# Scans that take the carry over 257 columns, gated outputs loaded during their projection, other waits in the background jobs, and first operands prepared one at a time

## The chip, the cores and the metric

The kernel runs on one core of one Trainium2 chip. A core has five engines with instruction queues of their own: TensorE for matrix products (PE in the profile, its weight loads PEld), VectorE (DVE), ScalarE (ACT), GpSimd (POOL) and SyncE (SP), which here issues nearly all DMA transfers. An engine works through its own queue in order and waits at an instruction until the data and buffers it needs are free. The metric is the time of the program on the device in microseconds (us), the median of several runs; lower is better.

## The reference

One decoder layer on a sequence of 1024 positions and 2048 channels, all in float32. It normalizes `x`, projects it with `w_in` to 6656 columns, and runs two groups of 16 heads of width 64: stick-breaking attention (`sb`) and sliding-window attention with four key/value heads, a position bias and a sink (`sw`). Each group's output is normalized over its 1024 columns, multiplied by a gain and by `silu(z)` of its own gate projection, and both together go through `w_out`, a norm and the residual.

```python
# stick breaking, for s < t:
A[t, s] = sigmoid(z_ts) * prod_{s < j < t} (1 - sigmoid(z_tj))
# the layer
u = rmsnorm(h, norm_pre)
q_sb, k_sb, v_sb, z_sb, q_sw, k_sw, v_sw, z_sw = split(u @ w_in)
o_sb = rmsnorm(stick_breaking(q_sb, k_sb, v_sb), gn_sb) * silu(z_sb)
o_sw = rmsnorm(sliding_window(q_sw, k_sw, v_sw, sinks, rel_bias), gn_sw) * silu(z_sw)
y = concatenate([o_sb, o_sw]) @ w_out
h = h + rmsnorm(y, norm_post)
```

The sequence is stored back to front, so the product over later keys in the reference becomes a running product from left to right: a scan.

## The kernel before

**Precision.** A float32 product is made from three faster ones: each operand is split into a high part (a cast on ScalarE, L133, L545, L747, L774) and the rest (a subtraction on VectorE, L135, L546, L748, L775), and TensorE adds high by high, high by low and low by high (L122, L872).

**Phase 1: projections.** `w_in` is cut into 52 blocks of 128 columns. `proj` (L435) makes one: four groups `kg` of four 128-row tiles, for both halves `h` of the 1024 positions, 96 matmuls of 512 columns. The list `work` (L700) fixes their order: window heads first, then queries, keys and values of the eight stick-breaking pairs with the gate projections `z_sw` and `z_sb` between them, and at the end six `z_sb` alone. After each block its `done` function empties the accumulators.

**Attention in between.** After every few matmuls `proj` calls `step` (L252), which starts at most one piece of attention (`advance`, L152) and then lets the background jobs go on. A unit of stick-breaking attention (`unit_sb`, L495) covers 256 queries, as two blocks of 128, by 256 keys: its first part computes logits, the two sigmoids into `m` and `beta` (L515, L517), and two scans over 256 columns (L526), one per block of queries. The tile `m` has 257 columns; column 0 is the running product so far. In the first unit of a row of units GpSimd sets it to 1 (L520); in every later one GpSimd copies it from column 256 of the unit before (L524). Then `beta` is multiplied by `m` shifted by one column (L530). The second part transposes on TensorE (L537, L126) and splits; the third multiplies by the values, and the output goes to the tensors `od` in device memory.

**The gate.** `evac_z` (L404) ends a z projection. For each half it loads the attention output from `od` (two parts, L408, one buffer with the tag `or`), adds the parts on GpSimd (L410), computes `silu(z)` times the gain (L366, L413, L414), multiplies by the output (L415), squares the output on GpSimd and adds that to the group's sum (L419, L421, L422), and stores the product to `ogd` (L423). `group_rms` (L425) turns the sum into one over the root mean square, in rows of 512 positions (L430, L431); for the window heads that happens 12 planner-microseconds after the last `z_sw`, for the others during the first product of phase 2.

**Background jobs.** 80 `sum_job`s add or subtract blocks of `w_out` (two loads, one operation on GpSimd, one store); eight `scale_job`s then multiply the gated window outputs by their norm row, store that to `ogs`, subtract the halves and store that to `w21`. Two chains run them, one in a tile `bg`, one in `row_sw` until that tile is needed for the norm. The number after each `yield` is the least time until the job's next step.

**What sets the order.** The program counts `pe_time`, the time TensorE should have needed for the matmuls written so far; `defer`, the lags of the units and the waits of the jobs are all in these planner-microseconds. Matmuls of phase 1 and the steps of background jobs keep their written order; other instructions are ordered on their engines by a scheduler that simulates them when the program is built, with earlier-written ones preferred.

**Phase 2.** The output projection is done as seven products of quarter matrices (the idea of Strassen and Winograd), each over `e = 0..7` and two column halves `dc`. Its first operands are the scaled window outputs: `open_ph2` (L781), called before the last two projections, finishes what is deferred and all background jobs, frees the tiles of phase 1, and prepares all eight operands: `x_source` (L753) loads one from `ogs`, with two buffers, and `x_split` (L771) splits it. The weights are loaded by `load_wo` (L720) and split by `split_wo` (L731), the first eight with two buffers for the parts.

## Time and profile before

| | |
|---|---|
| median of 3 runs | 1875.68 us (1872.5 to 1877.07) |
| the profiled execution | 1870.6 us, span of its instructions 1868.9 us |
| mean granted TensorE clock | 0.987 |
| TensorE busy | 1794.2 us, 96% of the span |
| VectorE, ScalarE, GpSimd busy | 1263.6, 772.7 and 586.6 us |
| HBM traffic | 219.42 MB read, 91.23 MB written |

In a row of the profile, L526 is line 526 of the kernel; `m_sb<-m_sb,zero` names what is written and what is read; x192 counts instructions. In a timeline the first two numbers are the start and the duration in us, and the bracket at the end tells how long the engine had been idle and whose work ended that. SPq stands for SP's queue issuing a transfer. PEclk is the clock that TensorE was granted, as a share of full speed. A busy TensorE can still be slow, when the clock is low.

### The profile page before, as it was taken

The numbers are of one execution on the slowest core, as the hardware profiler recorded it, in microseconds if no ns is written. First come the engines' busy times: TensorE is split into PE (matmuls) and PEld (weight loads), VectorE is DVE, ScalarE is ACT, GpSimd is POOL, SyncE is SP. The second block draws the span as 40 slices with busy tenths as digits, with TensorE's granted clock in tenths as the row PEclk, the third lists the DMA queues.
The fourth block names the chain that finished last, engine by engine and source line by source line (L and its number), as shares of the span: only waits on it lengthen the run. The fifth ranks groups of instructions, "written<-read, shape, count | busy, mean of one in ns | idle before, by whom it ended". The sixth has DMA issues, their size and how long they took to land. (4 is left out here: it accounts for less than half of the span.)

```text
span 1868.9 us, 27447 instructions
## 1 busy us (share of the span) xinstructions
PE 1794.2 (96%) x9046; PEld 1498.4 (80%) x9046; DVE 1263.6 (68%) x1976; ACT 772.7 (41%) x1664; POOL 586.6 (31%) x680
## 2 busy tenths in 40 slices
PE   8999999999999999999999989999999958999997
PEld 7788888878888878887888868888878846888886
DVE  7568842888387686785776767767688536655776
ACT  7345521445244343442433425434344214434432
POOL 0111121112234253253342332223444553403623
PEclk9999999999999999999999999999999979999999
DMA  7546775566646465555555553544534477534475
GB/s 228 195 141 189 200 211 149 159 191 201 201 142 177 139 186 169 167 156 157 161 168 164 155 161 106 151 120 144 157 110 141 134 243 240 163 108 136 135 246 188
DMA packets 205421, 312.50 MB, mean 167 GB/s; under 512 B 26176, under 2 KB 85728, under 8 KB 205152
## 3 DMA queue, kind: packets, MB, share of 16 engines
q1 hardware_dynamic: 203216, 307.61, 54.9%
q10 hardware_dynamic: 2064, 3.15, 0.5%
q8 instruction: 72, 1.18, 0.3%
q14 instruction: 69, 0.57, 0.1%
HBM read 219.42 MB, written 91.23 MB: 166 GB/s over the span
## 5 line engine op out<-in xcount | busy, mean ns | idle before, releaser
L526 DVE TENSOR_TENSOR_SCAN m_sb<-m_sb,zero 128x256 f32<-128x256 f32 x192 | 165.0, 900 | 47.3 <-ACT m_sb L515 45.5
L872 PE MATMUL y<-wohi,x 128*128 128x512 f32 x448 | 144.3, 399 | 15.1 <-ACT x L774 13.5
L515 ACT ACTIVATE m_sb<-z_sb 128x512 f32<-128x512 f32 x160 | 96.2, 601 | 147.4 <-PE z_sb L122 136.0
L521 POOL TENSOR_SCALAR_AFFINE_SELECT b_sb<-b_sb 128x512 f32<-128x512 f32 x64 | 48.9, 764 | 328.0 <-ACT b_sb L517 325.9
L530 DVE TENSOR_TENSOR b_sb<-b_sb,m_sb 128x512 f32<-128x512 f32 x160 | 137.3, 858 | 19.2 <-POOL b_sb L521 7.1
L545 ACT CAST wh_sb<-wt_sb 128x512 fp32r<-128x512 f32 (+1 forms) x160 | 87.1, 544 | 130.4 <-PE wt_sb L126 130.0
L526 DVE TENSOR_TENSOR_SCAN m_sb<-m_sb,mask 128x256 f32<-128x256 f32 x128 | 114.3, 929 | 38.8 <-ACT m_sb L515 38.1
L872 PE MATMUL y<-wohl,x 128*128 128x512 f32 x576 | 132.8, 389 | 1.5 <-DVE wohl L748 1.5
L546 DVE TENSOR_TENSOR wl_sb<-wt_sb,wh_sb 128x512 fp32r<-128x512 f32 (+1 forms) x160 | 100.5, 630 | 47.8 <-ACT wh_sb L545 47.4
L872 PEld LDWEIGHTS y<-wohl,x 128*128 128x128 f32 x576 | 108.0, 188 | 24.3 <-DVE wohl L748 1.9
L872 PEld LDWEIGHTS y<-wohi,x 128*128 128x128 f32 x448 | 86.2, 193 | 34.8 <-ACT x L774 13.9
L122 PE MATMUL p_zsb<-xh,wlo_zsb 128*128 128x512 f32 x256 | 101.7, 397 | 5.4 <-DVE wlo_zsb L135 5.4
L122 PE MATMUL p_vsb<-xh,wlo_vsb 128*128 128x512 f32 x256 | 101.5, 397 | 5.0 <-DVE wlo_vsb L135 5.0
L122 PE MATMUL p_ksb<-xh,whi_ksb 128*128 128x512 f32 x256 | 104.4, 408 | 0.4 <-ACT whi_ksb L133 0.4
L122 PE MATMUL p_zsw<-xh,whi_zsw 128*128 128x512 f32 x256 | 104.7, 409 | 0.0
L122 PE MATMUL p_qsb<-xh,whi_qsb 128*128 128x512 f32 x256 | 104.6, 409 | 0.0
L122 PE MATMUL p_zsb<-xh,whi_zsb 128*128 128x512 f32 x256 | 103.9, 406 | 0.0
L122 PE MATMUL p_vsb<-xh,whi_vsb 128*128 128x512 f32 x256 | 103.9, 406 | 0.0
L126 PE MATMUL wt_sb<-ident,b_sb 128*128 128x128 f32 x576 | 89.5, 273 | 14.0 <-DVE b_sb L530 14.0
L126 PEld LDWEIGHTS wt_sb<-ident,b_sb 128*128 128x128 f32 x576 | 72.4, 141 | 37.9 <-issue 17.6
L122 PE MATMUL p_zsw<-xh,wlo_zsw 128*128 128x512 f32 x256 | 101.4, 396 | 0.0
L122 PE MATMUL p_vsb<-xl,whi_vsb 128*128 128x512 f32 x256 | 101.3, 396 | 0.0
(243 smaller groups left out, 5125.8 us busy)
## 6 DMA issues: line engine op xcount, KB each, us to landing
bg<-in_w_out SPq DMA_DIRECT2D x86, 256.0 KB, 4.2
woraw<-wsum SPq DMA_DIRECT2D x80, 256.0 KB, 3.2
row_sw<-in_w_out SPq DMA_DIRECT2D x74, 256.0 KB, 4.5
wsum<-bg SPq DMA_DIRECT2D x43, 256.0 KB, 2.6
kh<-kd SPq DMA_DIRECT2D x160, 64.0 KB, 2.8
kl<-kd SPq DMA_DIRECT2D x160, 64.0 KB, 2.7
wsum<-row_sw SPq DMA_DIRECT2D x37, 256.0 KB, 2.6
q_sw<-qd SPq DMA_DIRECT2D x64, 128.0 KB, 3.3
```

Source lines behind the costliest of these rows:

```text
L122: tc.keep_in_program_order(nc.tensor.matmul(ps, a, b, start=start, stop=stop))
L126: tc.keep_in_program_order(nc.tensor.transpose(ps, a, ident))
L515: nc.scalar.activation(m[:, :, 1:257], z, AF.Sigmoid, scale=-SCALE)
L521: nc.gpsimd.affine_select(out=beta, in_=beta, compare_op=ALU.is_gt, fill=0.0, base=0, pattern=[[-P, 2], [1, 256]], channel_multiplier=-1)
L526: nc.vector.tensor_tensor_scan(m[:, tb, 1:257], m[:, tb, 1:257], mask[:, P - P * tb:P - P * tb + 256] if prev is None else zero.to_broadca ...
L530: nc.vector.tensor_mul(beta, beta, m[:, :, 0:256])
L545: nc.scalar.copy(wh[:, :k], pt[:, :k])
L546: nc.vector.tensor_sub(wl[:, :k], pt[:, :k], wh[:, :k].bitcast(F32))
L872: nc.tensor.matmul(ps, xt[:, a, tcols], w[b][:, cols], start=first and n == 0, stop=last and n == 2)
```

## The change

- `unit_sb`: column 0 of `m` is set to 1 in every unit. Where there is a unit before, the scan runs over all 257 columns and starts from that unit's last column, so GpSimd copies nothing.
- `evac_z`: the load and the addition of the first half move into the projection, ahead of its third group of weights (`mid`, `early`). The second half is loaded once the first has been used, and its multiplication, squares and store are deferred by 6 planner-microseconds, except in the last projection. The squares move from GpSimd to ScalarE.
- `group_rms` makes both products first and hands back the reciprocals as pieces: eight of 128 columns for the window heads, deferred one by one; four of 256 for the others, second half first, one for each `e` from 3 to 6. Its call in phase 2 moves from `e == 3` to `e == 2`.
- Background jobs: waits of 8, 6 and 6 in place of 9, 6 and 7 in a `sum_job`; 7, 4, 4, 4, 4 in place of 9, 6, 7, 6, 7 in a `scale_job`; the chains begin at 112 and 122 in place of 130 and 140. The scale jobs are queued 14.5 planner-microseconds after the window heads' norm.
- Phase 2: the eight first operands become a background job (`prepare_x0`) with a wait of 5 between loads, finished after the last projection.

```diff
@@ -223,31 +223,31 @@
         def run(t):
             BG(nc.sync.dma_start(t[:, 0, :], w_view(a, e, cols)))
             BG(nc.sync.dma_start(t[:, 1, :], w_view(b, e, cols)))
-            yield 9.0
+            yield 8.0
             BG((nc.gpsimd.tensor_add if sign > 0 else nc.gpsimd.tensor_sub)(t[:, 0, :], t[:, 0, :], t[:, 1, :]))
             yield 6.0
             BG(nc.sync.dma_start(wsum[i][e][:, cols], t[:, 0, :]))
-            yield 7.0
+            yield 6.0
...
     def scale_job(e):
         def run(t):
             f = t.rearrange("p a n -> p (a n)")
             BG(nc.sync.dma_start(f, ogd[8 + e]))
-            yield 9.0
+            yield 7.0
             BG(nc.gpsimd.tensor_mul(f, f, row_sw))
-            yield 6.0
+            yield 4.0
             BG(nc.sync.dma_start(ogs[e], f))
-            yield 7.0
+            yield 4.0
             BG(nc.gpsimd.tensor_sub(t[:, 0, :], t[:, 1, :], t[:, 0, :]))
-            yield 6.0
+            yield 4.0
             BG(nc.sync.dma_start(w21[e], t[:, 0, :]))
-            yield 7.0
+            yield 4.0
         return run
 
     jobs.extend(sum_job(i, e, dc) for i in W_SUMS for dc in range(2) for e in range(8))
-    open_chain(row_sw, 130.0)
-    open_chain(at.tile([P, 2 * HALF], F32, tag="bg", name="bg", bufs=1), 140.0)
+    open_chain(row_sw, 112.0)
+    open_chain(at.tile([P, 2 * HALF], F32, tag="bg", name="bg", bufs=1), 122.0)
 
...
@@ -401,38 +401,53 @@
 
     accs = {}
 
-    def evac_z(ps, name, tile_i, gain, grp):
+    early_o = {}
+
+    def load_o(name, tile_i, h):
+        o2 = stg.tile([P, 2, HALF], F32, tag="or", name=f"or_{name}_{h}", bufs=1)
+        nc.sync.dma_start(o2, od[tile_i][:, :, h * HALF:(h + 1) * HALF].rearrange("r p t -> p r t"))
+        nc.gpsimd.tensor_add(o2[:, 0, :], o2[:, 0, :], o2[:, 1, :])
+        return o2[:, 0, :]
+
+    def evac_z(ps, name, tile_i, gain, grp, last=False):
+        zf, sg = [], []
         for h in range(2):
+            zf.append(scaled(ps[h], name, h))
+            sg.append(stg.tile([P, HALF], F32, tag="sg", name=f"sg_{name}_{h}"))
+            nc.scalar.activation(sg[h], zf[h], AF.Sigmoid)
+            nc.vector.scalar_tensor_tensor(zf[h], zf[h], gain, sg[h], op0=ALU.mult, op1=ALU.mult)
+        if tile_i % 8 == 0:
+            accs[grp] = stg.tile([P, S], F32, tag="acc", name=f"acc_{grp}", bufs=1)
+
+        def gate(h, o):
             cols = slice(h * HALF, (h + 1) * HALF)
-            o2 = stg.tile([P, 2, HALF], F32, tag="or", name=f"or_{name}_{h}", bufs=1)
-            nc.sync.dma_start(o2, od[tile_i][:, :, cols].rearrange("r p t -> p r t"))
-            o = o2[:, 0, :]
-            nc.gpsimd.tensor_add(o, o, o2[:, 1, :])
-            zf = scaled(ps[h], name, h)
-            sg = stg.tile([P, HALF], F32, tag="sg", name=f"sg_{name}_{h}")
-            nc.scalar.activation(sg, zf, AF.Sigmoid)
-            nc.vector.scalar_tensor_tensor(zf, zf, gain, sg, op0=ALU.mult, op1=ALU.mult)
-            nc.vector.tensor_mul(zf, zf, o)
+            nc.vector.tensor_mul(zf[h], zf[h], o)
+            nc.sync.dma_start(ogd[tile_i][:, cols], zf[h])
             if tile_i % 8 == 0:
-                if h == 0:
-                    accs[grp] = stg.tile([P, S], F32, tag="acc", name=f"acc_{grp}", bufs=1)
-                nc.gpsimd.tensor_mul(accs[grp][:, cols], o, o)
+                nc.scalar.square(accs[grp][:, cols], o)
             else:
-                nc.gpsimd.tensor_mul(sg, o, o)
-                nc.gpsimd.tensor_add(accs[grp][:, cols], accs[grp][:, cols], sg)
-            nc.sync.dma_start(ogd[tile_i][:, cols], zf)
-
-    def group_rms(grp, row):
-        for h in range(2):
+                nc.scalar.square(sg[h], o)
+                nc.gpsimd.tensor_add(accs[grp][:, cols], accs[grp][:, cols], sg[h])
+
+        gate(0, early_o.pop(name))
+        o1 = load_o(name, tile_i, 1)
+        if last:
+            gate(1, o1)
+        else:
+            defer(6.0, lambda: gate(1, o1))
+
+    def group_rms(grp, row, width, order=(0, 1)):
+        ps = {h: pz(f"rms_{grp}_{h}") for h in order}
+        for h in order:
             cols = slice(h * HALF, (h + 1) * HALF)
-            ps = pz(f"rms_{grp}_{h}")
-            mm(ps, ones, accs[grp][:, cols], start=True, stop=True)
-            nc.scalar.activation(row[:, cols], ps, AF.Sqrt, bias=eps, scale=1.0 / 1024)
-            nc.vector.reciprocal(row[:, cols], row[:, cols])
+            mm(ps[h], ones, accs[grp][:, cols], start=True, stop=True)
+            nc.scalar.activation(row[:, cols], ps[h], AF.Sqrt, bias=eps, scale=1.0 / 1024)
+        parts = [row[:, h * HALF + c:h * HALF + c + width] for h in order for c in range(0, HALF, width)]
+        return [lambda r=r: nc.vector.reciprocal(r, r) for r in parts]
 
...
-    def proj(b, name, nxt=None):
+    def proj(b, name, nxt=None, mid=None):
...
@@ -441,6 +456,8 @@
         ps = [pproj(f"p_{name}_{h}") for h in range(2)]
         for kg in range(4):
             wh, wl = splits.pop(0)
+            if kg == 2 and mid is not None:
+                mid()
             if kg < 3:
                 splits.append(get(b, name, kg + 1))
             elif nxt is not None:
@@ -516,16 +533,17 @@
             beta = at.tile([P, 2, 256], F32, tag="beta", name=f"b_{un}", bufs=3)
             nc.scalar.activation(beta, z, AF.Sigmoid, scale=SCALE)
             prev = grp.get("prev")
+            nc.gpsimd.memset(m[:, :, 0:1], 1.0)
             if prev is None:
-                nc.gpsimd.memset(m[:, :, 0:1], 1.0)
                 nc.gpsimd.affine_select(out=beta, in_=beta, compare_op=ALU.is_gt, fill=0.0, base=0,
                                         pattern=[[-P, 2], [1, 256]], channel_multiplier=-1)
-            else:
-                nc.gpsimd.tensor_copy(m[:, :, 0:1], prev[:, :, 256:257])
             for tb in range(2):
-                nc.vector.tensor_tensor_scan(m[:, tb, 1:257], m[:, tb, 1:257],
-                                             mask[:, P - P * tb:P - P * tb + 256] if prev is None else zero.to_broadcast([P, 256]),
-                                             m[:, tb, 0:1], ALU.mult, ALU.max)
+                if prev is None:
+                    nc.vector.tensor_tensor_scan(m[:, tb, 1:257], m[:, tb, 1:257], mask[:, P - P * tb:P - P * tb + 256],
+                                                 m[:, tb, 0:1], ALU.mult, ALU.max)
+                else:
+                    nc.vector.tensor_tensor_scan(m[:, tb, :], m[:, tb, :], zero.to_broadcast([P, 257]),
+                                                 prev[:, tb, 256:257], ALU.mult, ALU.max)
             grp["prev"] = m
             nc.vector.tensor_mul(beta, beta, m[:, :, 0:256])
             me["w"] = beta
@@ -675,16 +693,25 @@
             if p == 7:
                 def rms():
                     close_chain(chains[0])
-                    group_rms("sw", row_sw)
-                    jobs.extend(scale_job(e) for e in range(8))
+                    for n, piece in enumerate(group_rms("sw", row_sw, 128)):
+                        defer(2.0 + 1.5 * n, piece)
+                    defer(14.5, lambda: jobs.extend(scale_job(e) for e in range(8)))
                 defer(12.0, rms)
         return f
 
     def done_z_sb(p):
         def f(ps):
-            drain(f"sb{p}")
-            evac_z(ps, f"zsb{p}", p, gsb[:, p:p + 1], "sb")
+            evac_z(ps, f"zsb{p}", p, gsb[:, p:p + 1], "sb", p == NPAIR - 1)
         return f
+
+    def early(name, tile_i):
+        def f():
+            assert not left.get(f"sb{tile_i}", 0)
+            early_o[name] = load_o(name, tile_i, 0)
+        return f
+
+    mids = {f"zsw{p}": early(f"zsw{p}", 8 + p) for p in range(NPAIR)}
+    mids.update({f"zsb{p}": early(f"zsb{p}", p) for p in range(NPAIR)})
 
...
@@ -785,13 +812,22 @@
         ph2.append(ctx.enter_context(tc.tile_pool(name="at2", bufs=2, reuse_waits="tile")))
         ph2.append(ph2[0].tile([P, D], F32, tag="gp", name="gp", bufs=1))
         nc.sync.dma_start(ph2[1], g_post.partition_broadcast(P))
-        xs.extend(x_split(0, e, x_source(0, e)) for e in range(8))
+        chains.append(dict(buf=None, at=pe_time[0], job=prepare_x0()))
+
+    def prepare_x0():
+        src = []
+        for e in range(8):
+            src.append(x_source(0, e))
+            if e:
+                xs.append(x_split(0, e - 1, src[e - 1]))
+            yield 5.0
+        xs.append(x_split(0, 7, src[7]))
 
     for n, (b, name, done) in enumerate(work):
         nxt = work[n + 1][:2] if n + 1 < len(work) else None
...
-        ps = proj(b, name, nxt)
+        ps = proj(b, name, nxt, mids.get(name))
         if n == len(work) - 3:
             drain(f"sb{NPAIR - 1}")
         if nxt is None:
@@ -800,6 +836,7 @@
         if n == len(work) - 3:
             open_ph2()
 
+    background(True)
     at2, gp = ph2
     row_sb = rstd
 
@@ -896,8 +933,10 @@
                 split_wo(k0 + e + 6)
                 for tb in range(4):
                     mm_out(pss[tb], xs[e], tb, w_ready[k0 + e], whole, e == 0, e == 7)
-                if i == 0 and dc == 0 and e == 3:
-                    group_rms("sb", row_sb)
+                if i == 0 and dc == 0 and e == 2:
+                    pieces_rms = group_rms("sb", row_sb, 256, (1, 0))
+                if i == 0 and dc == 0 and 2 < e < 7:
+                    pieces_rms[e - 3]()
                 if i == 0 and dc == 1:
                     load_b(1, e)
                 if i == 1 and dc == 0:
```

## The prediction

> **What bounds the kernel now.** I read first the page's busy shares, then the list of what TensorE waited for, then stretches of one fortieth of the span.
>
> ```profile
> span 1868.9 us, 27447 instructions
> PE 1794.2 (96%) x9046; PEld 1498.4 (80%) x9046; DVE 1263.6 (68%) x1976; ACT 772.7 (41%) x1664; POOL 586.6 (31%) x680
> ...
> PE wt_sb L126 <- DVE b_sb L530: 14.0, 7, 3.6
> PE y L872 <- ACT x L774: 13.5, 1, 13.5
> ...
> PE p_zsb L122 <- DVE wlo_zsb L135: 5.4, 1, 5.4
> PE o_sb L122 <- DVE wl_sb L546: 5.2, 6, 1.7
> PE y L872 <- DVE wolo L748: 5.0, 2, 4.7
> PE p_vsb L122 <- DVE wlo_vsb L135: 5.0, 1, 5.0
> ```
>
> TensorE runs 96% of the span and the change leaves its matmuls as they are, so only TensorE's idle time, and the slow matmuls after it, can be won. These six rows, all in stages that the change touches, sum to 48.1 us. How much the idle time costs beyond itself is in the granted clock:
>
> ```profile
> 654.10:700.80 46.70, 43.51 (x229) 36.51 (x228) 39.35 (x49) 19.61 (x38) 24.77 (x31) 0.96 0.65 186
> 840.90:887.70 46.80, 43.21 (x215) 36.04 (x214) 27.84 (x38) 13.99 (x28) 15.56 (x22) 0.96 0.52 157
> 1074.60:1121.30 46.70, 40.18 (x191) 32.38 (x190) 29.29 (x31) 13.49 (x24) 16.85 (x21) 0.93 0.54 161
> ...
> 1495.10:1541.80 46.70, 27.10 (x98) 20.95 (x98) 14.32 (x20) 7.99 (x13) 23.55 (x16) 0.75 0.72 244
> 1541.80:1588.60 46.80, 40.88 (x159) 31.43 (x158) 31.93 (x27) 21.81 (x38) 18.66 (x12) 0.92 0.74 239
> 1588.60:1635.30 46.70, 46.70 (x207) 38.66 (x206) 30.14 (x34) 18.96 (x34) 21.91 (x14) 1.00 0.53 163
> ```
>
> The columns are the stretch, its length, then busy time and count of PE, PEld, DVE, ACT, POOL, then the TensorE clock, DMA share and GB/s. A stretch of undisturbed 512-column matmuls holds 207 of them, 46.7 / 207 = 0.226 us each. The two stretches around the change of phase hold 98 and 159: (109 + 48) x 0.226 = **35.4 us** lost there, the slow clock included. In the stick-breaking stage the clock of 0.96, 0.96 and 0.93 costs about 0.04 x 46.7 = 1.9, 1.9 and 0.07 x 46.7 = 3.3 us more than the waits.
>
> **Part 1, the gate of each z projection.** One of the sixteen, in DVE's, POOL's and PE's order of time:
>
> ```profile
> 841.59 0.72 DVE L414 SCALAR_TENSOR_TENSOR u_zsw<-u_zsw,gsw,sg_zsw 128x512 f32<-128x512 f32 x1
> ...
> 848.63 0.69 DVE L415 TENSOR_TENSOR u_zsw<-u_zsw,or_zsw 128x512 f32<-128x512 f32 x1 [5.12 <-POOL or_zsw L410]
> 849.24 3.13 DVE L526 TENSOR_TENSOR_SCAN m_sb<-m_sb,zero 128x256 f32<-128x256 f32 x2
> ...
> 847.31 1.29 POOL L410 TENSOR_TENSOR or_zsw<-or_zsw 128x512 f32<-128x512 f32 x1 [4.67 <-DMA or_zsw<-od]
> 848.68 1.55 POOL L421 TENSOR_TENSOR sg_zsw<-or_zsw 128x512 f32<-128x512 f32 x1
> ...
> 853.32 0.45 PE L126 MATMUL wt_sb<-ident,b_sb 128*128 128x128 f32 x1 [3.59 <-DVE b_sb L530]
> ...
> L526 DVE TENSOR_TENSOR_SCAN m_sb<-m_sb,zero x192: 718/742/1776, 518.0 to 1452.8; 128x256 f32<-128x256 f32 x192
> ...
> or_zsw<-od SPq DMA_DIRECT2D x16, 512.0 KB, 5.4
> ...
> L300 ACT ACTIVATE xsq<-xraw 128x512 f32<-128x512 f32 x30 | 17.8, 623 | 4.0 <-DVE acc_x L301 4.0
> L133 ACT CAST whi_zsb<-wraw_zsb 128x512 fp32r<-128x512 f32 x32 | 19.9, 622 | 41.0 <-PE p_zsb L122 30.0 <-issue 5.1 <-PE p_vsb L122 2.8
> ```
>
> The second half's load cannot start until the first half leaves the one `or` buffer. DVE reaches the second gate, stands 5.12 us, and all behind it is late; then its two scans take 3.13 us in place of 2 x 0.742 while POOL squares beside them; PE stops for 3.59 us. The wait list's 14.0 + 5.2 us are mostly stalls of this shape. With the two clock losses of 1.9 this term holds 19.2 + 3.8 = **23 us**.
>
> The change loads the first half in mid-projection, squares on ACT, and puts the second gate 6 planner-microseconds later. One planner-microsecond is about 1.19 us here (worked out in part 2), so the second gate stands about 7.1 us after the projection. In the rows above it was ready 848.63 - 841.59 = 7.0 us after the second half's silu, which itself comes some 2 us, three operations of about 0.7, behind the projection's end: a gate as late as this, the worst of its kind, still waits about 2 of its 5.1 us; with the load's median of 5.4 us most others are covered. I take a quarter left, **17 us won**; the bounds are 0 (the gate stands before its data as often as today) and 23.
>
> What the edit adds is behind TensorE: 32 squares on ACT, 0.62 us each by the row of x's squares, 20 us on an engine 41% busy, and taken off POOL. The early load of 512 KB goes to SP ahead of a quarter's weight loads; the cast row of the z weights names no wait for their load among its three longest, so it costs nothing while that lead lasts. If each of the 16 made one quarter's weights 2 us late it would be 32 us; I take 0. What is queued behind the new waiting instruction matters more: the second half's square now sits in ACT's order, with the weight casts behind it. Where the load is late, ACT stops as well as DVE.
>
> **Part 2, the pace of the weight sums, and the group norm of the window heads.**
>
> ```profile
> L227 POOL TENSOR_TENSOR bg<-bg x43: 1262/1296/1777, 168.2 to 1273.5; 128x512 f32<-128x512 f32 x43
> L227 POOL TENSOR_TENSOR row_sw<-row_sw x37: 1285/1303/1752, 154.5 to 1094.8; 128x512 f32<-128x512 f32 x37
> L238 POOL TENSOR_TENSOR bg<-bg,row_sw x8: 2346/2400/2772, 1293.6 to 1518.8; 128x1024 f32<-128x1024 f32 x8
> ...
> 1103.95 3.34 DVE L431 RECIPROCAL row_sw<-row_sw 128x512 f32<-128x512 f32 x1
> ...
> 1108.59 0.80 PE L122 MATMUL p_vsb<-xh,wlo_vsb 128*128 128x512 f32 x1 [5.03 <-DVE wlo_vsb L135]
> ```
>
> One chain made 37 sums, 36 steps of 9 + 6 + 7 = 22 planner-microseconds, in 1094.8 - 154.5 = 940.3 us: 26.1 us a step, hence 26.1 / 22 = 1.19. At 20 a step takes 23.7 us; begun 18 x 1.19 = 21 us earlier, both chains fit 2 x (940 + 21) / 23.7 = 81 sums before 1095, where 80 are wanted. So the eight scale jobs no longer queue behind sums until 1273.5: they start near 1115 (the change gives the norm 14.5 planner-microseconds first) and, at 23 planner-microseconds (27 us) each in place of 35, end near 1335 rather than in the last two projections (the last multiply is at 1518.8). By itself this moves nothing on TensorE's path; it is what frees part 3. Denser sums may add or save a microsecond in the window stage: -1 to +3, taken as 0.
>
> The norm's reciprocal is split into eight pieces of 3.34 / 4 = 0.84 us, spread apart. The term is the wait of 5.03 and 3.3 of clock, 8.3 us. ACT's table load and roots stay, and a piece can still push a split: I leave 2.3, about three pieces, **6 won**; bounds 0 and 8.3.
>
> **Part 3, the end of the projections and the first product.**
>
> ```profile
> 1507.83 0.69 DVE L415 TENSOR_TENSOR u_zsb<-u_zsb,or_zsb 128x512 f32<-128x512 f32 x1 [10.79 <-POOL or_zsb L410]
> ...
> 1526.16 0.32 SPq L244 DMA_DIRECT2D w<-bg  x1
> ...
> 1528.61 0.92 SPq L765 DMA_DIRECT2D xs<-ogs  x2
> ...
> 1536.00 1.27 ACT L774 CAST x<-xs 128x512 fp32r<-128x512 f32 x2 [5.62 <-DMA xs<-ogs]
> ...
> 1536.67 0.80 PE L872 MATMUL y<-wohi,x 128*128 128x512 f32 x1 [13.53 <-ACT x L774]
> 1557.55 0.50 PE L872 MATMUL y<-wohi,x 128*128 128x512 f32 x1 [0.88 <-ACT wohi L747]
> ...
> 1534.23 0.69 DVE L415 TENSOR_TENSOR u_zsb<-u_zsb,or_zsb 128x512 f32<-128x512 f32 x1 [4.37 <-POOL or_zsb L410]
> ...
> 1566.45 6.57 DVE L431 RECIPROCAL rstd<-rstd 128x512 f32<-128x512 f32 x2 [3.92 <-ACT rstd L430]
> ```
>
> Today the last scale jobs are forced out at the end, the last store of theirs, at 1526.16, stands ahead in SP's queue, the first x operand is asked for at 1528.61, and TensorE waits 13.53 us and then crawls at a lower clock as x pairs trickle in. The stall of 10.79 us is a gate behind POOL's scale jobs and makes the 5.4 us in the first list. After the change the scale jobs are long done; the eight x operands are asked for one every 5 planner-microseconds, 40 in all, and the two projections that remain are 2 x 96 x 0.226 = 43 us of TensorE's time. So the first product starts as the projections end.
>
> What is late next: the weight splits of the first product have two buffers, so one lasts 12 x 0.226 = 2.7 us. The wait for wohi (0.88) and the wolo that followed it (5.0 - 4.7 = 0.3) stay, 1.2. The last gate is not deferred: today's wait of 4.37 less the 2.7 us in hand is 1.7, and I allow as much again for a lower clock. The 6.57 us of reciprocal become four pieces of 1.64 with splits between them: 1.5. Together about 6 of the 35.4 stay: **29 us won**; bounds 19 (the 1.2, a gate's wait of 4.4 and the reciprocal's of 4.7 as today, each with 3 of clock, are 16 left) and 34.
>
> **Part 4, the scan.**
>
> ```profile
> L524 POOL COPY m_sb<-m_sb 128x2 f32<-128x2 f32 x96 | 50.1, 522 | 117.8 <-DVE m_sb L526 105.7 <-ACT wh_sb L545 8.8 <-ACT b_sb L517 2.6
> ...
> L520 POOL MEMSET m_sb<- x64: 93/98/109, 1.9 to 1453.9; 128x2 f32 x64
> ```
>
> One more column is 742 / 256 = 3 ns on 192 scans, 0.6 us of DVE. POOL loses 50.1 us of copies and gains 96 x 0.098 = 9.4 of memsets. More to the point, POOL no longer stands in its order for the scan before (105.7 us), so its adds for the gates come sooner. None of it is on TensorE's path alone: 0, bounds 0 and +2 of gain, within part 1.
>
> **The sum.** 17 + 6 + 29 = 52 us off the profiled execution's 1870.6 (its span 1868.9 and 1.7 around it): 1818.6. That execution lies 5.1 us under the median of the runs, 1875.68; against the median I expect 1875.7 - 52 = 1823.7, **1824**.
>
> **The rivals.**
>
> *More comes.* Nothing of the stalls stays but the first weights' 1.2: 23 + 8.3 + 34.2 = 65.5, **1810**. For it: every one of the waits has its named cause removed. Against: the order on the engines is replanned, and a plan's loads are faster than the 5.4 us seen here. 15%.
>
> *The wait of the second half stays.* The deferred gates still stand before their data, now ACT with DVE: part 1 gives 4, part 3 its lower bound of 19: 4 + 6 + 19 = 29, **1847**. For it: 4.67 us of POOL's waiting for that load above, and one buffer still. Against: the 7.1 us of delay. 21%.
>
> *The operands are not ready after all.* The sums just miss 1095 (81 places for 80), or the buffers of the second phase come free only with the last units, so x is prepared at the end as today; half of part 3 goes: 17 + 6 + 14.5 = 37.5, **1838**. 9%.
>
> *ACT changes tables for each square* (slower than before). The profile's table loads:
>
> ```profile
> L515 ACT ACT_TABLE_LOAD x2 | 2.6, 1283 | 0.0
> ```
>
> If squares need another table than the sigmoids on both sides of them, each costs ACT two loads, 2 x 1.283 = 2.57 us, in front of the sigmoids and casts that feed PE. 28 of the 32 squares lie ahead of the last two projections, among stick-breaking units; DVE's stall of 5.12 gave PE 3.59, so the 2.57 would give 1.8 and, more often than before, a clock loss; at 2.57 a square, 28 x 2.57 = 72 against the 52 won: **1896**. It decides from 52 / 28 = 1.9 us a square. Against it: L300 squares x at the start, and no load carries that line. 4%. [...]
>
> **How the numbers follow.** The forecast, 1815 to 1833, has 46%; the rivals 15, 21, 9 and 4; another 5% lies around no change (4) or worse (1), by weights late behind the early loads or a worse plan. The range 1808 to 1850 takes in the first three rivals and leaves out the slower cases and some of the tails, under 20%. A measurement of this kernel tells about 0.3%, 5.6 us, from no change. Faster by more 91%, within 4%, slower 5%.
>
> **What would show it.** In the changed profile: the wait of y for ACT's x (13.5) gone and both 46.7 us stretches near 200 matmuls; the last multiply by `row_sw` before 1350; the gate's multiply without a wait on POOL's add over 2 us except at the last projection; table loads still seven; no PE wait of 5 us after the window norm. I am wrong if the first product still waits over 5 us, if PE's waits for b_sb and wl_sb stay above 10, or if ACT waits at the new squares.

## The result, and the profile after

Over four runs each, the changed kernel takes 1820.97 us at the median (1817.14 to 1825.41) and the kernel before 1874.09 (1870.83 to 1877.07): a ratio of **0.9718**, 95% interval 0.9689 to 0.9746, or 53 us less. The forecast was 1824. The profiled execution of the new kernel is the longest of its four, 1825.41 us; so its span, 1823.7 us, lies 45.2 us under the span before, and not 53.

The page of the kernel after, and its list of what TensorE waited for (total, times, longest):

```profile
PE 1786.3 (98%) x9046; PEld 1493.2 (82%) x9046; DVE 1242.3 (68%) x1984; ACT 787.2 (43%) x1696; POOL 496.2 (27%) x648
...
PE wt_sb L126 <- DVE b_sb L548: 3.0, 2, 2.0
...
PE o_sb L122 <- DVE wl_sb L564: 2.4, 2, 1.2
...
PE y L909 <- DVE wolo L775: 1.8, 2, 1.5
PE p_zsb L122 <- ACT whi_zsb L133: 1.4, 1, 1.4
PE p_zsb L122 <- DVE wlo_zsb L135: 1.3, 2, 0.7
```

The six waits on which the forecast was built summed to 48.1 us. The waits for `b_sb` and `wl_sb` are now 5.4 (19.2 before), those of the last projections for their weights 2.7 (5.4), `wolo` 1.8 (5.0). The wait of the first product for `x` (13.5) and that of `p_vsb` (5.0) are not in the list any more. The prediction's stretches but the last, which was undisturbed before too, now of the kernel after:

```profile
654.10:700.80 46.70, 44.73 (x238) 37.86 (x237) 39.24 (x49) 22.43 (x44) 19.14 (x30) 0.96 0.63 177
840.90:887.70 46.80, 46.80 (x244) 39.53 (x243) 29.16 (x42) 16.50 (x33) 12.84 (x23) 1.00 0.60 178
1074.60:1121.30 46.70, 46.70 (x238) 38.70 (x237) 34.62 (x49) 20.27 (x37) 12.44 (x22) 1.00 0.46 142
1495.10:1541.80 46.70, 44.41 (x189) 34.70 (x188) 27.38 (x29) 22.05 (x39) 14.01 (x10) 1.00 0.73 244
1541.80:1588.60 46.80, 46.80 (x208) 38.77 (x207) 37.90 (x38) 19.79 (x36) 29.02 (x20) 1.00 0.57 185
```

The clock is 1.00 in four of five, and the two stretches around the change of phase hold 189 and 208 matmuls in place of 98 and 159. The timeline around the first product:

```profile
1499.82 0.39 PE L122 MATMUL p_zsb<-xh,wlo_zsb 128*128 128x512 f32 x1
1500.05 0.39 PE L909 MATMUL y<-wohi,x 128*128 128x512 f32 x1
```

The scale jobs, the sigmoids' table loads and the new squares (count, duration in ns, first and last start):

```profile
L238 POOL TENSOR_TENSOR bg<-bg,row_sw x8: 2394/2500/2942, 1096.9 to 1295.1; 128x1024 f32<-128x1024 f32 x8
...
L532 ACT ACT_TABLE_LOAD  x2: 1283/1283/1283, 517.1 to 1107.5; - x2
...
L429 ACT ACTIVATE sg_zsw<-or_zsw x14: 631/632/636, 598.3 to 1079.1; 128x512 f32<-128x512 f32 x14
```

The first product starts at 1500.05 in place of 1536.67, one matmul behind the projections. That divides the profiled gain of 45.2 us: 13.5 is the wait itself, 36.6 - 13.5 = 23.1 was won ahead of it, and 45.2 - 36.6 = 8.6 behind it. The scale jobs end with a multiply at 1295.1 (1518.8 before). The new squares cost 0.63 us each. Between the sigmoids' two table loads, at 517.1 and 1107.5, fourteen of them run; the profile has seven table loads in all, as before, and none stands on a line of the squares.

Below, a difference between two kernels is the difference of their ratios to the kernel before, times 1874 us.

### The profile page after: what moved, and what is told of

Read it like the earlier page. It is cut to its first block, busy times and chain, and to the rows that moved or that the text cites. A ratio compares the mean times of both kernels' runs of the same rounds, so it can differ in the third digit from the quotient of the medians.

```text
span 1823.7 us, 27416 instructions
## 1 busy us (share of the span) xinstructions
PE 1786.3 (98%) x9046; PEld 1493.2 (82%) x9046; DVE 1242.3 (68%) x1984; ACT 787.2 (43%) x1696; POOL 496.2 (27%) x648
## 5 line engine op out<-in xcount | busy, mean ns | idle before, releaser
L545 DVE TENSOR_TENSOR_SCAN m_sb<-m_sb,m_sb,zero 128x257 f32<-128x257 f32 x192 | 159.9, 871 | 49.9 <-ACT m_sb L532 46.8
L548 DVE TENSOR_TENSOR b_sb<-b_sb,m_sb 128x512 f32<-128x512 f32 x160 | 128.3, 802 | 25.2 <-POOL b_sb L538 13.8
L542 DVE TENSOR_TENSOR_SCAN m_sb<-m_sb,mask 128x256 f32<-128x256 f32 x128 | 119.0, 967 | 38.6 <-ACT m_sb L532 36.9
L909 PEld LDWEIGHTS y<-wohl,x 128*128 128x128 f32 x576 | 109.2, 190 | 25.7 <-DVE wohl L775 2.9
L122 PE MATMUL p_zsw<-xl,whi_zsw 128*128 128x512 f32 x256 | 101.1, 395 | 0.0
L122 PE MATMUL p_ksb<-xh,wlo_ksb 128*128 128x512 f32 x256 | 101.1, 395 | 0.0
L122 PE MATMUL p_zsb<-xl,whi_zsb 128*128 128x512 f32 x256 | 101.1, 395 | 0.0
L122 PE MATMUL p_qsb<-xh,wlo_qsb 128*128 128x512 f32 x256 | 100.8, 394 | 0.0
L122 PE MATMUL p_ksb<-xl,whi_ksb 128*128 128x512 f32 x256 | 100.8, 394 | 0.0
```

Source lines behind the costliest of these rows:

```text
L122: tc.keep_in_program_order(nc.tensor.matmul(ps, a, b, start=start, stop=stop))
L542: nc.vector.tensor_tensor_scan(m[:, tb, 1:257], m[:, tb, 1:257], mask[:, P - P * tb:P - P * tb + 256], m[:, tb, 0:1], ALU.mult, ALU.max)
L545: nc.vector.tensor_tensor_scan(m[:, tb, :], m[:, tb, :], zero.to_broadcast([P, 257]), prev[:, tb, 256:257], ALU.mult, ALU.max)
L548: nc.vector.tensor_mul(beta, beta, m[:, :, 0:256])
L909: nc.tensor.matmul(ps, xt[:, a, tcols], w[b][:, cols], start=first and n == 0, stop=last and n == 2)
```

## Experiments: the pace, and the operands

**The old pace in the kernel after** (all waits and starts of the jobs as they were):

```diff
-            yield 8.0
+            yield 9.0
...
-            yield 6.0
+            yield 7.0
...
-    open_chain(row_sw, 112.0)
+    open_chain(row_sw, 130.0)
-    open_chain(at.tile([P, 2 * HALF], F32, tag="bg", name="bg", bufs=1), 122.0)
+    open_chain(at.tile([P, 2 * HALF], F32, tag="bg", name="bg", bufs=1), 140.0)
...
-                    defer(14.5, lambda: jobs.extend(scale_job(e) for e in range(8)))
+                    jobs.extend(scale_job(e) for e in range(8))
```

> The changed kernel, but with the old waits and starts of the background jobs (9, 6, 7 and 9, 6, 7, 6, 7, begun at 130 and 140, scale jobs queued at once after the window norm). Theory A: scale jobs again run into the last two projections, most of part 3 comes back, +18 to +29, 1840 to 1850; the last multiply by row_sw falls within 60 us of the first product. Rival B (step by step is what pays): +0 to +6. Rival C (denser sums cost the window stage some 4 us): the stage up to 500 us gets faster by 3 to 5 us.

Measured: 1838.9 us, ratio 0.9815 (0.9793 to 0.9836), so 18 us of the gain are gone, the low end of what was expected. Its timeline on TensorE:

```profile
1512.67 0.80 PE L909 MATMUL y<-wohi,x 128*128 128x512 f32 x1 [20.95 <-ACT x L801]
```

And its scale jobs:

```profile
L238 POOL TENSOR_TENSOR bg<-bg,row_sw x8: 2337/2400/2832, 1272.8 to 1494.2; 128x1024 f32<-128x1024 f32 x8
```

The multiplies run to 1494.2 again and the first product waits for its first operand, although that operand is asked for by the new job. **All operands asked for at once, in the kernel after:**

```diff
-        chains.append(dict(buf=None, at=pe_time[0], job=prepare_x0()))
+        xs.extend(x_split(0, e, x_source(0, e)) for e in range(8))
```

> The changed kernel, but with the eight first operands of phase 2 asked for all at once when phase 1's tiles are freed, as before; all else changed. Theory A (the operands were late because SP's queue and the stores it waits for were held by the last scale jobs; asking one at a time only spreads them): the same as the changed kernel within 4 us, about 1822 us, and the first product starts without a wait over 2 us. Rival B (asking all at once blocks SP's queue behind two buffers, so the step-by-step job is what pays): half or more of the 29 us of part 3 comes back, 1836 to 1850, with TensorE waiting over 5 us before the first product.

Measured: 1821.74 us, 0.9724 (0.9689 to 0.9759), the same as after. TensorE has no wait for `x`. **And the step-by-step operands alone, in the kernel before** (the same lines the other way round):

> The kernel before with the first operands prepared one at a time alone. Theory A: they still stand behind the scale jobs, within 5 us of before, 1870 to 1880, TensorE's wait for ACT's x still over 10 us. Rival B: 10 us or more faster.

Measured: 1873.47 us, 1.0009 (0.9995 to 1.0022): nothing, and the first product waits 14.9 us. The new way of asking is worth nothing in either kernel.

**The new pace in the kernel before** (the waits and starts of the first diff the other way round, and the operands step by step, which change nothing by themselves):

> The kernel before with the new waits and starts of the background jobs alone. Theory A (the pace frees the end of the projections and the first product, and with it the gate that stood behind a scale job there): 20 to 30 us faster than before, 1845 to 1855, and TensorE's wait for the first operand under 3 us. Rival (pace helps only with the other parts): under 10 us faster.

Measured: 1854.73 us, 0.9903 (0.9886 to 0.992), 18 us faster, just short of the 20 to 30 expected. In its list of waits:

```profile
PE wt_sb L126 <- DVE b_sb L532: 13.9, 8, 3.4
PE y L886 <- DVE wolo L752: 7.5, 3, 4.7
PE o_sb L122 <- DVE wl_sb L548: 7.4, 5, 2.2
...
PE p_vsb L122 <- DVE wlo_vsb L135: 1.1, 1, 1.1
```

The gates' waits are there as before (13.9 + 7.4 for 14.0 + 5.2), and so is the reciprocal's in the first product (4.7). But the wait behind the window heads' norm fell from 5.0 to 1.1, although its reciprocals are whole here. Why is not shown.

## Experiments: the gate

**The old gate in the kernel after** (load at the end, no deferral, squares on GpSimd, all of `evac_z` as it was):

> The changed kernel with the old gate: both halves loaded after the projection, gates not deferred, squares on GpSimd. My theory: PE's waits for b_sb and wl_sb, 5.4 us in the changed profile, go back to 15 or more, and the time by +12 to +17, 1833 to 1838. Rival (the gate's stalls were made by GpSimd standing for the scan and by scale jobs, which stay away): +5 or less.

Measured: 1831.72 us, 0.9774 (0.9751 to 0.9797): 10.5 us, a little less than expected. From its list of TensorE's waits:

```profile
PE o_sb L122 <- DVE wl_sb L550: 8.4, 6, 2.2
...
PE wt_sb L126 <- DVE b_sb L534: 5.3, 6, 2.0
```

TensorE's two waits are 13.7, where the kernel after has 5.4. But VectorE stands at this gate's multiply (L415) for GpSimd for only 17.9 us in all, against 43.9 in the kernel before and 25.7 in the kernel after (L424 there): with the other edits in place the old gate is less late than the new one, and yet TensorE stops more. So its cost is not the late load.

**The new gate in the kernel before** (that edit the other way round):

> The kernel before with the new gate alone. Undone one by one, pace costs 18, gate 11 and norms 13 us, 42 of the 53 won. If the rest is a stall that either the pace or the gate removes (the gate behind a scale job at 1507 us, 5.4 us and the slow clock after it, about 8), the gate alone wins 16 to 21 us, 1853 to 1858. Rival (the rest is noise or comes of the parts together): 8 to 13 us, 1861 to 1866.

Measured: 1858.45 us, 0.9919 (0.9894 to 0.9944), 15 us faster: between the two ranges, so it decides for neither. From its list of waits:

```profile
PE y L906 <- ACT x L798: 20.4, 1, 20.4
PE wt_sb L126 <- DVE b_sb L546: 10.2, 6, 3.1
...
PE o_sb L122 <- DVE wl_sb L562: 1.6, 2, 0.9
```

The wait for `x` grows from 13.5 to 20.4, as the projections end sooner: what the gate wins ahead of it is partly given back there. The gate's waits fall from 19.2 to 11.8 and do not go away. The stall of 5.4 us behind a scale job, which my expectation named, is gone from the list.

**The kernel after, squares back on GpSimd, all else new:**

```diff
-                nc.scalar.square(accs[grp][:, cols], o)
+                nc.gpsimd.tensor_mul(accs[grp][:, cols], o, o)
-                nc.scalar.square(sg[h], o)
+                nc.gpsimd.tensor_mul(sg[h], o, o)
```

> The changed kernel with the squares of the gate left on GpSimd; loads and deferral as changed. My theory: GpSimd's squares stand beside VectorE's scans and lengthen them, the mean of a 257-column scan goes from 0.87 to about 0.90 us, and TensorE loses little: +1 to +4 us. Rival (the move to ScalarE is what shortens the stall): +7 or more. Rival (ScalarE, now waiting for the load in its order, loses as much as GpSimd gains): -3 to 0.

Measured: 1841.3 us, 0.983 (0.9812 to 0.9847): 21 us slower than after, and slower than the whole old gate. My theory, that the squares matter little, fell; the first rival, +7 or more, holds. Two rows of its list of TensorE's waits:

```profile
PE wt_sb L126 <- DVE b_sb L548: 7.4, 6, 3.4
...
PE o_sb L122 <- DVE wl_sb L564: 4.9, 3, 2.0
```

The timeline of one gate in it, on VectorE, GpSimd and TensorE:

```profile
662.82 0.69 DVE L424 TENSOR_TENSOR u_zsw<-u_zsw,or_zsw 128x512 f32<-128x512 f32 x1 [2.34 <-POOL m_sb L536]
663.43 3.13 DVE L545 TENSOR_TENSOR_SCAN m_sb<-m_sb,m_sb,zero 128x257 f32<-128x257 f32 x2
...
662.87 1.54 POOL L429 TENSOR_TENSOR sg_zsw<-or_zsw 128x512 f32<-128x512 f32 x1
664.49 1.52 POOL L430 TENSOR_TENSOR acc_sw<-acc_sw,sg_zsw 128x512 f32<-128x512 f32 x1
...
668.31 1.08 PE L126 MATMUL wt_sb<-ident,b_sb 128*128 128x128 f32 x4 [3.39 <-DVE b_sb L548]
```

And the same gate in the kernel after:

```profile
664.71 0.69 DVE L424 TENSOR_TENSOR u_zsw<-u_zsw,or_zsw 128x512 f32<-128x512 f32 x1 [2.13 <-POOL m_sb L536]
665.32 2.39 DVE L545 TENSOR_TENSOR_SCAN m_sb<-m_sb,m_sb,zero 128x257 f32<-128x257 f32 x2
...
665.43 1.73 POOL L430 TENSOR_TENSOR acc_sw<-acc_sw,sg_zsw 128x512 f32<-128x512 f32 x1 [0.71 <-ACT sg_zsw L429]
...
669.46 0.93 PE L126 MATMUL wt_sb<-ident,b_sb 128*128 128x128 f32 x4 [1.98 <-DVE b_sb L548]
```

Both gates wait about as long (2.34 and 2.13 us), so it is not the load that differs. What differs stands behind the gate: two scans beside two GpSimd operations take 3.13 us, beside one 2.39, and TensorE stops for 3.39 or 1.98 us. The same holds over the run. The scans that carry on from a unit, first with the squares on GpSimd, then in the kernel after (busy time and mean ns behind the bar):

```profile
L545 DVE TENSOR_TENSOR_SCAN m_sb<-m_sb,m_sb,zero 128x257 f32<-128x257 f32 x192 | 172.1, 934 | 45.3 <-ACT m_sb L532 42.2 <-POOL m_sb L536 2.4
...
L545 DVE TENSOR_TENSOR_SCAN m_sb<-m_sb,m_sb,zero 128x257 f32<-128x257 f32 x192 | 159.9, 871 | 49.9 <-ACT m_sb L532 46.8 <-POOL m_sb L536 2.7
```

VectorE as a whole is 26 us busier with the squares on GpSimd (1268.3 for 1242.3). It does not wait longer: the rows of its list of waits that name GpSimd sum to 44.5 us, for 53.5 in the kernel after. Why an instruction of VectorE takes longer while GpSimd squares is not shown; that its scans do is (934 ns for 871 at the mean). The squares on ScalarE took 0.631 to 0.636 us. The two profiled executions lie 11.5 us apart (1836.91 and 1825.41). Of that, 12.3 - 5.4 = 6.9 are in the waits for `b_sb` and `wl_sb` (7.4 + 4.9 here); and the mean granted clock is 0.993 here and 0.996 in the kernel after, which over the span of 1835 us is about 0.003 x 1835 = 5.5 more (the clocks are rounded to 0.001). The rest of the 21 us is in executions without a trace, where the clock was 0.991 and 0.992 for 0.997 and 0.998. Why it is slower than the old gate, which has the same squares, stays open.

**The old gate in the kernel after, squares on ScalarE** (the edit of the old gate above, but `nc.scalar.square` for both squares), and **the second gate written at once** (`gate(1, o1)` in place of its `defer`), and **deferred longer** (9.0 for 6.0, the norm at 14.0 for 12.0):

> The changed kernel with the old gate (both loads after the projection, no deferral) but its squares on ScalarE. If the engine of the squares is what the gate's gain rests on, as the run with the squares left on GpSimd suggests: within 4 us of the changed kernel, 1818 to 1826, TensorE's waits for b_sb and wl_sb under 8 us. If the early load and the deferral carry it: as slow as with the whole old gate, 1829 to 1835, and ScalarE now waits for the loads with the weight casts behind it.

> The changed kernel with the second gate written at once, not 6 planner-microseconds later. If the deferral counts: +4 to +10, with the gate's waits on GpSimd's addition (17.9 us of VectorE in the changed profile) at 30 or more. If the scheduler that orders the engines finds as good a place by itself: within 3 us of the changed kernel.

> The changed kernel with the second gate 9 planner-microseconds later in place of 6, and the window heads' norm at 14 in place of 12. The waits of VectorE and ScalarE for the second half's addition fall below a third, TensorE's waits near 669, 702, 820 and 1486 us go, with a slow clock after two of them: 5 to 8 us faster than the changed kernel, 1813 to 1816. Rival: the second half's buffer is freed too late for the next projection's early load, and nothing is gained, -2 to +3.

Measured: 1816.82 us, 0.9695 (0.968 to 0.9709) with the old loads; 1818.0, 0.97 (0.9686 to 0.9714) without the deferral; 1821.92, 0.9722 (0.9703 to 0.974) with a longer one, which was expected to win 5 to 8 and wins nothing. None is clearly slower than after. The waits of the first, with the old loads:

```profile
PE o_sb L122 <- DVE wl_sb L550: 3.6, 3, 2.2
...
PE wt_sb L126 <- DVE b_sb L534: 1.7, 2, 1.1
```

The two gate waits are 5.3 us, as in the kernel after (5.4). Between this kernel and the one with the whole old gate only the squares' engine differs: 0.9774 - 0.9695 = 0.0079, 15 us. Again VectorE is busier with the squares on GpSimd, 1276.6 for 1242.7, and waits no longer for it, 42.1 for 46.9. So four kernels, alike in all else, cross the two parts of the gate:

| | squares on GpSimd | squares on ScalarE |
|---|---|---|
| old loads, no deferral | 0.9774 | 0.9695 |
| new loads and deferral | 0.9830 | 0.9718 |

The squares' move wins 15 us in the first row and 21 in the second. In the kernel after it carries the gate's whole gain, and neither the early load nor the deferral is needed: with the squares on GpSimd they cost 10.5 us (the intervals lie apart), with the squares on ScalarE 4, where the intervals just overlap. In the kernel before, the squares' move was not tried alone, so the 15 us of the new gate there are not divided.

## Experiments: the norms, and the scan

**Whole reciprocals in the kernel after:**

```diff
-                    for n, piece in enumerate(group_rms("sw", row_sw, 128)):
-                        defer(2.0 + 1.5 * n, piece)
+                    group_rms("sw", row_sw)
-                if i == 0 and dc == 0 and e == 2:
-                    pieces_rms = group_rms("sb", row_sb, 256, (1, 0))
-                if i == 0 and dc == 0 and 2 < e < 7:
-                    pieces_rms[e - 3]()
+                if i == 0 and dc == 0 and e == 3:
+                    group_rms("sb", row_sb)
```

> The changed kernel with the old group norms: two reciprocals of 512 columns in one piece, for both groups. My theory: the waits of 5.03 and 4.73 us behind the reciprocals return with a slow clock after each, 8 at the window heads' norm and 6 to 8 in the first product: +10 to +16, 1831 to 1837. Rival (the reciprocals hurt only because the engine was late for other reasons that are gone): +5 or less.

Measured: 1833.97 us, 0.9787 (0.9771 to 0.9804), 13 us, as expected. But not where I had put half of it. Its list of TensorE's waits holds for the window heads' norm:

```profile
PE p_vsb L122 <- DVE wlo_vsb L135: 0.6, 1, 0.6
```

The timeline at the other norm, on VectorE and TensorE:

```profile
1524.31 6.57 DVE L445 RECIPROCAL rstd<-rstd 128x512 f32<-128x512 f32 x2 [3.92 <-ACT rstd L444]
...
1532.11 0.79 PE L907 MATMUL y<-wolo,x 128*128 128x512 f32 x1 [4.73 <-DVE wolo L773]
```

The window heads' norm costs TensorE 0.6 us; nearly all that the trace shows is in phase 2. There the weight split stands behind 6.57 us of reciprocal, TensorE stops for 4.73 and then gets 0.71 of its clock for five more (1532 to 1537). That is 4.73 + 0.29 x 5 = 6.2 of the 13. The profiled execution, 1828.9 us, is the fastest of its four; the others had a clock of 0.992, 0.992 and 0.993 where this one had 0.996, and where they lost the rest is not recorded. The timeline of the kernel after, at that place:

```profile
1527.71 1.75 DVE L446 RECIPROCAL rstd<-rstd 128x256 f32<-128x256 f32 x1 [3.92 <-ACT rstd L444]
1529.38 0.63 DVE L775 TENSOR_TENSOR wolo<-woraw,wohi 128x512 fp32r<-128x512 f32 x1
1529.93 4.96 DVE L446 RECIPROCAL rstd<-rstd 128x256 f32<-128x256 f32 x3
```

One split goes in after the first piece, and the other three pieces run in one go. That is enough: TensorE does not stop.

**The copied carry in the kernel after:**

```diff
+                nc.gpsimd.tensor_copy(m[:, :, 0:1], prev[:, :, 256:257])
-                    nc.vector.tensor_tensor_scan(m[:, tb, :], m[:, tb, :], zero.to_broadcast([P, 257]),
-                                                 prev[:, tb, 256:257], ALU.mult, ALU.max)
+                nc.vector.tensor_tensor_scan(m[:, tb, 1:257], m[:, tb, 1:257], zero.to_broadcast([P, 256]),
+                                             m[:, tb, 0:1], ALU.mult, ALU.max)
```

> The changed kernel with the copied carry and scans of 256 columns. My theory: nothing on TensorE's path, within 3 us of the changed kernel. Rival (GpSimd, standing in its order for the scan before, delays the additions that the gates wait for): +4 to +10, with the wait of the gate's multiply for GpSimd's addition clearly longer.

Measured: 1819.7 us, 0.9712 (0.969 to 0.9735), as after. GpSimd copies again, and stands in its order for the scans; the group of copies, with busy time, mean ns, and the idle time before them, and the group of memsets in the kernel after, which has no copies:

```profile
L541 POOL COPY m_sb<-m_sb 128x2 f32<-128x2 f32 x96 | 51.9, 541 | 128.6 <-DVE m_sb L543 125.4 <-ACT wh_sb L562 2.5 <-DMA wraw_zsb<-in_w_blk 0.6
...
L536 POOL MEMSET m_sb<- 128x2 f32 x160 | 15.7, 102 | 159.1 <-DVE m_sb L545 146.6 <-ACT wh_sb L563 9.3 <-ACT whi_zsw L133 3.1
```

So the new scan did not free GpSimd: it now stands at the memsets, 146.6 us for VectorE's scans (125.4 at the copies), probably until a buffer of `m` is free, which is not shown. The multiply of the gate does wait longer with the copies, 34.1 us for 25.7, as the rival had it, but no time follows: 128.6 or 159.1 us of waiting on an engine that nobody waits for at that moment cost nothing.

## Why the prediction was right, and where its reasons were not

The time was right: 1824 forecast, 1821 measured. Undone one at a time, the edits cost 18 (pace), 13 (norms), 10.5 (gate), 1 (operands) and -1 (scan), together 42 of the 53 us. The other 11 may be stalls that either of two edits removes, as the one behind the window norm is; that they all are is not shown. That the sum fits is in part luck: two of its terms came from other steps than those given. Step by step:

- **What bounds it.** Right. TensorE's matmuls are the same 9046, and the gain came out of its named waits (48.1 to 9.9 in the profiles, 38 of the 45.2) and the clock behind them (0.987 to 0.996 at the mean).
- **Part 1, 17 us from the gate.** The size was a little high (10.5 undone, 15 done alone). The waits left, 5.4 us, are near the quarter of 19.2 that it left, but by luck, for the cause was wrong. The prediction credited the early load and the deferral, and took the squares on ScalarE for an addition that lies "behind TensorE". The row for the right reading was quoted: two scans took 3.13 us beside GpSimd's squares in place of 2 x 0.742. I read it as part of the late gate and not as the thing that the move takes away. The step that counted how long "a gate as late as this" still waits was about a wait that hardly matters: in the kernel after, the old loads with the squares on ScalarE leave TensorE the same 5.3 us.
- **The signals for part 1** failed in part. I wrote that the gate would not wait over 2 us on GpSimd's addition except at the last projection, and that I was wrong if ScalarE waited at the new squares. Both waits are there (VectorE's of 4.9 and 3.7 us, at 1458 and 1485, are ahead of the last gate), in the kernel after's list of waits:

```profile
ACT sg_zsw L429 <- POOL or_zsw L409: 23.5, 6, 4.8
DVE u_zsb L424 <- POOL or_zsb L409: 11.9, 5, 4.9
```

  And its timeline at one of them:

```profile
1485.27 0.63 ACT L429 ACTIVATE sg_zsb<-or_zsb 128x512 f32<-128x512 f32 x1 [5.96 <-POOL or_zsb L409]
1485.81 0.60 ACT L133 CAST whi_zsb<-wraw_zsb 128x512 fp32r<-128x512 f32 x1
...
1486.46 0.50 PE L122 MATMUL p_zsb<-xh,whi_zsb 128*128 128x512 f32 x1 [1.44 <-ACT whi_zsb L133]
...
1487.86 0.50 PE L122 MATMUL p_zsb<-xh,wlo_zsb 128*128 128x512 f32 x1 [0.67 <-DVE wlo_zsb L135]
```

  The mechanism I warned of is real: the cast of the next weights stands behind the waiting square, and TensorE stops for it. But it costs 1.44 us, 0.67 more where the subtraction from that cast is late, and about 1.7 of slow clock behind them (last section). That is all that TensorE's list has for casts of `z` weights; whether some of the 2.4 us for `wl_sb` come of it is not shown. As a criterion it was wrong: a wait off TensorE's path proves nothing until TensorE's own row shows it.
- **Part 2, the pace.** Right in what it does: the sums were done in time, and the last multiply was before 1350, at 1295.1. "It is what frees part 3" was right, with 18 us. Denser sums cost little: the scans that carry on begin at 520.9 us, 2.9 later than before (518.0) and 2.7 later than with the old pace in the kernel after (518.2), inside the bound of +3 but more than the 0 taken.
- **Part 2, the window norm, 6 us.** Mis-sized when seen alone. The wait is gone, but with whole reciprocals it is 0.6 us, and the pace alone brings it to 1.1.
- **Part 3, 29 us.** Near in sum, if single edits may be added: 18 with the pace and 13 with the norms, the last of which is almost all in this part, come to 31. The step that credited the operands "asked for one every 5" was wrong, since asking for all at once does the same once the scale jobs are done. And the 1.5 us left for four pieces "with splits between them" were too much: nothing stayed, though three of the pieces run in one go.
- **Part 4, 0.** Right in time. The step that GpSimd "no longer stands in its order for the scan before" was wrong: it stands 146.6 us for scans, at the memsets, where it was 105.7 at the copies.
- **The rivals.** The slower one, a table load for each square, fell: fourteen squares ran from 598.3 to 1079.1 us, with no table load from the sigmoids' at 517.1 to the roots' at 1084.8, and the loads are seven as before. "More comes", 1810, was not reached by any kernel here. "The second half's wait stays" came true as a wait and not as a time. The operands were ready.

## What to carry to other kernels

A helper engine's work can hurt by making the critical engine's instructions longer and not by making them wait, as here, where two scans took 3.13 us beside two operations of GpSimd and 2.39 beside one: compare one operation's duration alone and beside the helper, and try the helper's work on another engine. With the squares on ScalarE in place of GpSimd, VectorE was 26 us less busy here (1242.3 for 1268.3). A background job that ends just ahead of a phase change is worth finding first: a faster pace of such jobs was the largest part here. Undo every edit singly afterwards, since two of the five did nothing and a third worked for another reason than the one given.

## What was not expected of the hardware

How much a stall cost in clock was not set here by its length alone. In stretches of a few us (columns as in the prediction, the clock third from the end), the kernel after behind its stall of 1.98 us at 669.46 and, a little later than its stall of 1.44 us, at 1489:

```profile
669.40:673.00 3.60, 3.54 (x12) 2.99 (x13) 3.50 (x6) 0.59 (x1) 0.68 (x3) 0.53 0.93 278
...
1489.00:1492.00 3.00, 3.00 (x9) 2.32 (x8) 0.01 (x1) 0.00 (x0) 1.27 (x1) 0.50 0.86 305
```

and the kernel with the old loads and the squares on ScalarE, behind a stall of 2.15 us:

```profile
699.74 0.38 PE L122 MATMUL o_sb<-wl_sb,v_vsb 128*128 128x256 f32 x1 [2.15 <-DVE wl_sb L550]
...
699.70:703.00 3.30, 3.26 (x19) 2.81 (x20) 3.19 (x5) 0.89 (x2) 0.34 (x1) 1.00 0.94 304
```

The clock fell to half behind 1.98 us (0.53 in that stretch), and behind 1.44 with another 0.67 soon after it (0.50), and stayed whole behind 2.15 (1.00, and 1.00 in the 4 us after it). Taken in windows of 0.05 us, each of the two falls lasts 3.4 us at a clock of 0.50, from 669.64 and from 1488.84. What decides whether a stall is followed by a fall is not shown.

For an estimate from these three stalls: a stall cost itself, and where one such fall followed it, 0.5 x 3.4 = 1.7 us more; the longest of the three was followed by none.
